# Two-layer encoder trunk: four modulation products moved ahead of attention, and attention 0's norm factors and outputs stored from GpSimd's queue

## Chip, cores and metric

The kernel runs on one core of a Trainium2 chip. The time is device microseconds from launch to end, as the median of three runs. Five engines matter: TensorE (PE in the profile, with its weight loads as PEld), VectorE (DVE), ScalarE (ACT), GpSimd (POOL) and SyncE (SP), which here only issues transfers. Each engine works through its own queue in order. An instruction that waits for a semaphore holds up everything behind it on that engine, also when a transfer is all that the queue issues.

## What is computed

Two pre-norm layers on a sequence of 1024 rows of 1024 features, all in float32. Layer 0 is differential attention with 8 heads, layer 1 multi-head latent attention. Each layer's input is a normalised x, scaled and shifted by a modulation that a conditioning vector c gives; its output passes a gate that c gives as well. Cut to layer 0:

```python
mod = silu(c) @ ada_w + ada_b            # shift, scale, gate: 3 x 1024
h = rmsnorm(x, norm_g) * (1.0 + scale) + shift
q, k, v, z = split(h @ w_in)             # 4 x 1024 columns
q, k = rope(q), rope(k)                  # 16 sub-heads of 64
p = softmax(q1 @ k1.T) - lam * softmax(q2 @ k2.T)   # per head
o = rmsnorm(p @ v, subln_g) * (1 - lambda_init)
x = x + gate * ((o * silu(z)) @ w_out)
```

## The kernel before

**Precision and products.** A float32 operand is split into a high part (ScalarE's cast to float32r) and a low part (a subtraction), and a product is three matmuls: high by high, high by low, low by high (lines 178 to 180). Line 223 makes the high parts of streamed weights on ScalarE, line 224 the low parts on GpSimd. A "k step" is three such matmuls of 128x512.

**The order of layer 0.** First come the normalised input and the first half of the value projection. Then `z0_pair` runs three times: a seven-product (Strassen-like) scheme makes the Q and K projections of heads 2, 4 and 6 from four weight quarters and writes them to DRAM (`rS`); `product0` is one of the seven products, four k steps each. Beside it a list of small jobs, `side`, gives up one entry per k step (`side.tick`; an entry `None` is an empty step), and `side.flush` empties the list at once. In the second run (p == 1) the rotations (rope) of head 0's K and Q are put on this list by `add_jobs` on VectorE: four jobs, each a fetch, two multiplications by the cosine and sine tables, an addition (L390 to L394), a cast on ScalarE (`high`, L398), a subtraction (L403) and stores to `hS`.

At the end of the third run the weights of what follows are split: those of the first streamed projection (`w1`, lines 223 and 224) and the first eight of the second value half's weights (`split_v1`, lines 1077 and 1078), four of them with VectorE and four with GpSimd. Then sixteen k steps of the streamed projections run (`Z_PRE`), then eight value tiles of eight k steps each (`v0_tile`), the seventh with the first scores ahead of it, then attention 0, head by head. A head has eight slots: in each a `q_tile` of scores and softmax (two score matrices, VectorE's maxima at L456, ScalarE's exponentials, VectorE's combination at L1164), the transposes and value products of earlier slots (`Tail`), and three to five k steps of the projections of later heads. `bring` issues the loads of K, Q and V for the next half head; `load_q` has four transfers, two for each of `qa` and `qb` (L844).

**Modulation products.** One of layer 1's sixteen shift and scale columns is a 512 KB load of weights (`ada`) and one VectorE instruction with accumulation over 128x1024 elements (`mod_dot`, L480, "a dot" below). `MODS` says how many are written ahead of each of the eight value tiles: eight in all. The eight others and the eight of the layer's own gate are steps of `gate_steps0`, one of which is taken in every slot from the first of attention 0 on: with one empty step ahead, and the loads of the first two in the second step, the dots are the steps 3 to 18, that is those of heads 0 and 1 and two of head 2. Then follow the gated output weights. The loads share two buffers.

**The norm factors of a half head.** When a half head's values are complete, `close` scales them (`head_out`) and multiplies by the gate (GpSimd, L1226); in the next slot `rest` sums the squares on TensorE, three small VectorE instructions and a power on GpSimd make the factors `y`, 128x4 numbers. `bcast_rows` (line 461) stores them to DRAM (`bc_d`, L464) and reads them back, spread over all partitions (`bc_s`, L466): two transfers in SP's queue. Two slots later GpSimd multiplies the half head by them (`scale`, L1196), and two slots after that SP stores it (`store`, L1200) to `oF`, from which the output projection reads. `hooks` is the list of what is left for the next slot; `after_scores` runs it at its end.

**What sets the order of a queue.** The program is written in one order, but the framework places each engine's instructions and transfers itself: an instruction goes as soon as a plan of the times says that its data and buffers are ready and nothing earlier in the program wants the engine. So instructions written late can be placed early. `in_turn` keeps an instruction in written order among those of its engine that are so marked (from attention 0 on), `behind` and `issue_after` put it behind a given one.

Of the kernel before, what the change touches and what calls it, by code (L numbers as in the profile page):

```python
# [11 lines left out]
F32 = mybir.dt.float32  # L12
# [9 lines left out]
P = 128  # L22
# [4 lines left out]
HF = 512  # L27
# [15 lines left out]
SPL1 = 2  # L43
Z_PRE = 16
V_LATE = 6
MODS = (2, 2, 2, 2, 0, 0, 0, 0)
MODS_K = 0
V1_AT = (3, 3)
NORM_AT = 5
# [35 lines left out]
def trunk(ctx: ExitStack, tc: tile.TileContext, A, out):  # L85
    nc = tc.nc
    SP, PE, V, S, G = nc.sync, nc.tensor, nc.vector, nc.scalar, nc.gpsimd
# [40 lines left out]
    dr = pool(ctx, "dr", bufs=1, space=DRAM)  # L128
# [6 lines left out]
    oF = [dr.tile([NH, 2, P, HF], F32, name=f"oF{l}") for l in range(2)]  # L135
# [49 lines left out]
    def behind(eng):  # L185

        return tc.issue_after(mk[eng]) if eng in mk else nullcontext()

    def in_turn(ins):

        return tc.keep_in_program_order(ins) if mk else ins
# [123 lines left out]
    side = Side()  # L315
# [153 lines left out]
    def t3(ap_):  # L469
        return ap_.rearrange("p (t q) -> p t q", t=4)  # L470
# [26 lines left out]
    def gen_mods(load, c2):  # L497

        for n in range(sum(MODS) + MODS_K):
            src, bias, acc = mod_job(n)  # L500
# [143 lines left out]
    for f in range(2):  # L644
        fs = slice(f * HF, f * HF + HF)
        spread = PE.matmul(cb[:, fs], ones[0:1, :], crow[0:1, fs], start=True, stop=True).ins
# [375 lines left out]
    def z0_pair(p, late):  # L1022
        h, more = FRONT[p], p + 1 < len(FRONT)

        def out(kind, half, t):
            if not kind:
                S.mul(t, t, SC0)
            SP.dma_start(rS[kind][h][half], t)

        if p == 1:  # L1030
            side.flush()
            add_jobs([(kind, 0, half) for kind in (1, 0) for half in range(2)], V, 7)
        u = zt("zu")
        S.copy(u, product0(h0q(0, 0)))
        late(0)
        c_ = zt("z11")
        V.tensor_add(c_, product0(h0q(1, 0)), u)
        out(1, 0, c_)
        late(1)
        v = zt("zv")  # L1040
        S.copy(v, product0(h0q(1, 1)))
        V.tensor_add(u, product0(TK[2]), u)
        u5 = zt("zu5")
        V.tensor_add(u5, product0(TK[1]), u)
        V.tensor_add(v, v, u5)
        out(1, 1, v)
        acc = product0(TK[3])
        c_ = zt("z22")
        V.tensor_add(c_, acc, u5)
        V.tensor_add(u, acc, u)  # L1050
        out(0, 1, c_)
        late(2)
        V.tensor_add(u, product0(TK[4]), u)
        out(0, 0, u)
        late(3)

    def add_jobs(jobs, eng, rest=0):

        jobs = [rot_job(*j, eng) for j in jobs]
        side.add(jobs[0][0], None, None)  # L1060
        for a, b in zip(jobs, jobs[1:] + [[None]]):
            side.add(b[0], None, *a[1:], *[None] * rest)
# [10 lines left out]
    def split_v1(n, eng):  # L1073
        for _ in range(n):
            raw = wvraw.pop(0)
            h_, l_ = tk()
            S.copy(h_, raw)
            eng.tensor_sub(l_, raw, f32v(h_))
            wv1.append((h_, l_))
# [20 lines left out]
    def late(p, i):  # L1100
        if p + 1 < len(FRONT):
            if i < 2:
                z0_fetch(p + 1, ((i, 0), (i, 1)))
            if i == 3 and p + 2 == len(FRONT):
                fetch_v1(4, zrt)
            return
        if i == 0:
            pre.extend(raw_of(*ORDER0[0], f) for f in range(2))
        if i == 1:
            fetch_v1(4, zt)  # L1110
        if i == 2:
            for _ in range(2):
                for a, b in zip(w1, split_raw(pre.pop(0), 4)):
                    a += b
            split_v1(4, V)
        if i == 3:
            split_v1(4, G)

    pre, w1 = [], ([], [])
    for p in range(len(FRONT)):  # L1120
# [47 lines left out]
    for tt in range(8):  # L1168
        if tt == V_LATE:
            psum("ps2", sc=2, tr=1, pv=1)  # L1170
            zz0 = sm.tile([P, 4], F32, name="zz")
            first += [zz0, q_tile(0, 0, 0, zz0, a0a, lambda c: None if c else v0_tile(V_LATE, 1, wv1))]
        for _ in range(MODS[tt]):
            next(mods_g)
# [14 lines left out]

    def finish(o, y, l, h, half, dst, ap_, dgs):  # L1190

        if dst is None:
            b, rb = bcast_rows(ap_, y, "osq", 4)

            def scale():
                in_turn(G.tensor_mul(t3(o), t3(o), rb))  # L1196
                hooks.append(lambda: hooks.append(store))

            def store():
                SP.dma_start(oF[l][h, half], o)  # L1200

            if l == 0:
                hooks.append(lambda: hooks.append(scale))
            else:
                hooks.append(scale)
            return
        rb = bank("z", "rb") if l else Y[1]
        for j in range(4):
            js = slice(j * P, (j + 1) * P)
            S.mul(dgs[:, js], ident, y[:, j : j + 1])  # L1210
            PE.matmul(rb[:, js], ones, dgs[:, js], start=True, stop=True)
        V.tensor_mul(o, o, rb)
# [68 lines left out]
    tails, hooks = [None, None], []  # L1281
# [79 lines left out]
    def gate_steps0():  # L1361

        gcol = sm.tile([P, KT], F32, name="gcol", tag="gcol", bufs=1)
        yield
        w = []
        jobs = [mod_job(n) for n in range(sum(MODS) + MODS_K, 2 * KT)]
        late = len(jobs)
        jobs += [(A["ada_g0"][j], part("ada_bg0")[:, j : j + 1], gcol[:, j : j + 1]) for j in range(KT)]
        for n in range(len(jobs)):
            while len(w) < min(2, len(jobs) - n):  # L1370
                with tc.issue_after(mod_load.last):
                    w.append(mod_load(jobs[n + len(w)][0], pg, 2))
            yield
            with behind("V"):
                mod_dot(w.pop(0), *jobs[n][1:], c2)
                if n == late - 1:
                    g, _, _, a_, _ = mods[1]
                    V.scalar_tensor_tensor(out=a_, in0=a_, scalar=1.0, in1=g, op0=ALU.add, op1=ALU.mult)
        SP.dma_start(gateS[0].rearrange("(p j) -> p j", p=P), gcol)
        yield  # L1380
        SP.dma_start(c2, gateS[0][None, :].to_broadcast([P, D]))
        gb = c2[:, :HF], c2[:, HF:]

        def two(name):
            t = pg.tile([P, D], F32, name=name, tag="ada", bufs=2)
            return t[:, :HF], t[:, HF:]

        def put(*pairs):
            for n, t in pairs:
                SP.dma_start(tS[0][n, h], t)  # L1390

        for h in range(4):
            b_ = (b11, b12), (b21, b22) = two("ob1"), two("ob2")
            for m in range(2):
                for f in range(2):
                    SP.dma_start(b_[m][f], A["w_out0"][f, 4 * m + h])
                yield
            for m in range(2):
                for f in range(2):
                    in_turn(G.tensor_mul(b_[m][f], b_[m][f], gb[f]))  # L1400
                if m:
                    put((0, b11))
                yield
            put((1, b21), (4, b22))
            in_turn(G.tensor_sub(b12, b12, b11))
            t2 = a0c.tile([P, HF], F32, name="ot2", tag="ot2", bufs=2)
            in_turn(G.tensor_sub(t2, b22, b12))
            yield
            put((3, b12), (2, t2))
            in_turn(G.tensor_sub(b11, t2, b11))  # L1410
            in_turn(G.tensor_sub(b21, b21, t2))
            yield
            put((5, b11), (6, b21))
            yield
        for h, wait in ((0, 46), (1, 54)):
            while slot0 < wait:
                yield
            a_ = (a11, a12), (a21, a22) = two("oa1"), two("oa2")
            for m in range(2):
                for f in range(2):  # L1420
                    SP.dma_start(a_[m][f], oF[0][h + 4 * f, m])
                yield
            for _ in combine(a11, a12, a21, a22):
                yield
            SP.dma_start(sS[0][0, h], a22)
            SP.dma_start(sS[0][2, h], a21)
            yield
            SP.dma_start(sS[0][1, h], a11)
            SP.dma_start(sS[0][3, h], a12)
            yield  # L1430
# [94 lines left out]
    class Pre2:  # L1525
        n = 0
# [1049 lines left out]
    def scale(tt, y):  # L2576
        full, early = xs_[tt], tt // 4
        c1, c2_ = halves[early], halves[1 - early]

        def second():  # L2580
            V.scalar_tensor_tensor(out=full[:, c2_], in0=full[:, c2_], scalar=y, in1=fg[:, c2_], op0=ALU.mult, op1=ALU.mult)
            SP.dma_start(out[tt][:, c2_], full[:, c2_])

        def first_():
            S.mul(full[:, c1], full[:, c1], y)
            SP.dma_start(out[tt][:, c1], full[:, c1])

        if tt == NT - 2:
            held.extend((second, first_))
        else:  # L2590
            second()
            first_()
# [160 lines left out]
```

## Time and profile before

| | |
|---|---|
| median of three runs | 1418.11 us (1416.24 to 1419.38) |
| the profiled execution | 1416.81 us, its span 1414.9 us |
| mean granted TensorE clock | 0.991 |
| PE busy | 1369.7 us, 97% of the span |
| DVE / ACT / POOL busy | 1010.1 / 734.5 / 721.1 us |
| transfers | 282.41 MB, mean 200 GB/s |

The profile is of one execution. The times in it start at the span's start. The three `z0_pair` runs lie at about 106 to 171 us, the first streamed projections and the value tiles up to about 233 us, attention 0 from there to about 715 us, its output projection behind it, and layer 1 from about 830 us on. A row of the windows gives for each engine the busy time and the count of instructions in that stretch, a row of the timeline the start, the duration, the engine, the line and the operands, and in brackets the idle time ahead of it and what ended that. Queues that issue transfers have a q behind the engine's name.

### The profile page before, as it was taken

Reading aid. Unit: us, or ns where it says so; the run is one execution under the profiler, and the core shown is the slowest. Engines: PE = TensorE matmul, PEld = TensorE weight load, DVE = VectorE, ACT = ScalarE, POOL = GpSimd, SP = SyncE. Lnnn points to the kernel's source line nnn. Section 1 sums busy time; section 2 is a strip of 40 time slices with the busy share of each in tenths; the row PEclk is TensorE's granted clock in tenths of the full one; section 3 lists DMA queues with packets and bytes.
Section 4 is the critical chain, followed back from the end, with each engine's and each line's share of the span. In section 5 each row is a group of like instructions: output and inputs, shape, how many; then the busy total and the mean of one; then the engine's idle time right before and its main releaser. Section 6 shows DMA issues by size and latency. Waiting matters only on the chain.

```text
span 1414.9 us, 20936 instructions
## 1 busy us (share of the span) xinstructions
PE 1369.7 (97%) x7298; PEld 1141.1 (81%) x7298; DVE 1010.1 (71%) x1414; ACT 734.5 (52%) x1332; POOL 721.1 (51%) x574
## 2 busy tenths in 40 slices
PE   8998899998999999999999999999999999999997
PEld 6786688787888878887787788887888888888886
DVE  7789817999977867888687986645656655555684
ACT  5543314555666655565756553335454454545554
POOL 4424640565688775554785233533141273844673
PEclk8999999999999999999999999999999999999999
DMA  9835778687788776866574236498433354676463
GB/s 341 270 119 179 256 209 282 203 234 236 241 245 250 231 220 202 236 190 198 164 278 165 75 105 210 138 296 262 156 102 120 109 169 159 196 223 196 144 256 120
DMA packets 175243, 282.41 MB, mean 200 GB/s; under 512 B 23457, under 2 KB 60449, under 8 KB 175138
## 3 DMA queue, kind: packets, MB, share of 16 engines
q1 hardware_dynamic: 168610, 266.40, 60.3%
q10 hardware_dynamic: 4608, 8.39, 1.6%
q0 software_dynamic: 1920, 6.29, 1.2%
q8 instruction: 57, 0.93, 0.3%
q14 instruction: 48, 0.39, 0.1%
HBM read 182.49 MB, written 86.98 MB: 190 GB/s over the span
## 4 chain that ended last, share of the span: by engine, by line
PE 71%; DVE 13%; DMA 4%; issue 4%; ACT 4%; POOL 3%; SPq 1%; POOLq 0%; DVEq 0%; ACTq 0%
PE s L2367 10%; PE tr L439 7%; PE acc L180 7%; PE acc L179 6%; PE acc L178 6%; PE s L1156 6%; PE pv L179 4%; PE pv L178 4%; PE pv L180 4%; DVE ada L480 2%; DVE nm L456 2%; DVE e L1164 2%; PE zacc L180 1%; PE zacc L178 1%; PE zacc L179 1%
## 5 line engine op out<-in xcount | busy, mean ns | idle before, releaser
L441 ACT CAST pth<-tr 128x512 fp32r<-128x512 f32 x256 | 150.4, 587 | 247.7 <-PE tr L439 244.8
L442 DVE TENSOR_TENSOR ptl<-tr,pth 128x512 fp32r<-128x512 f32 x256 | 175.9, 687 | 134.5 <-ACT pth L441 129.2
L456 DVE TENSOR_REDUCE nm<-s 128x1 f32<-128x1024 f32 x192 | 233.5, 1217 | 22.0 <-PE s L1156 13.1
L224 POOL TENSOR_TENSOR wl<-wraw,wh 128x512 fp32r<-128x512 f32 (+2 forms) x65 | 84.6, 1302 | 274.5 <-ACT wh L223 249.2
L458 ACT ACTIVATE e<-s,nm 128x1024 f32<-128x1024 f32 x128 | 143.5, 1121 | 63.8 <-DVE nm L456 63.2
L439 PE MATMUL tr<-ident,e 128*128 128x128 f32 x1024 | 155.7, 274 | 8.2 <-DVE ptl L442 7.8
L439 PEld LDWEIGHTS tr<-ident,e 128*128 128x128 f32 x1024 | 120.8, 140 | 50.0 <-DVE ptl L442 28.0
L178 PE MATMUL pv<-pth,vt 128*128 128x256 f32 x512 | 147.8, 289 | 0.0
L179 PE MATMUL pv<-ptl,vt 128*128 128x256 f32 x512 | 147.1, 287 | 0.0
L180 PE MATMUL pv<-pth,vt 128*128 128x256 f32 x512 | 144.6, 282 | 0.0
L178 PE MATMUL acc<-h0h,wh 128*128 128x512 f32 x264 | 108.6, 411 | 0.0
L180 PE MATMUL acc<-h0h,wl 128*128 128x512 f32 x264 | 105.1, 398 | 2.8 <-POOL wl L224 2.8
L179 PE MATMUL acc<-h0l,wh 128*128 128x512 f32 x264 | 105.6, 400 | 0.0
L178 PEld LDWEIGHTS pv<-pth,vt 128*128 128x128 f32 x512 | 97.3, 190 | 3.2 <-ACT pth L441 0.8
L179 PEld LDWEIGHTS pv<-ptl,vt 128*128 128x128 f32 x512 | 97.5, 190 | 2.3 <-DVE ptl L442 0.3
L180 PEld LDWEIGHTS pv<-pth,vt 128*128 128x128 f32 x512 | 97.5, 191 | 0.4
L1503 POOL TENSOR_TENSOR wol<-wol,woh 128x512 fp32r<-128x512 f32 x56 | 82.4, 1494 | 25.5 <-ACT woh L1502 23.9
L1156 PE MATMUL s<-ks,qa 128*128 128x512 f32 x256 | 85.6, 415 | 7.4 <-DVE e L1164 7.1
L1156 PE MATMUL s<-ks,qb 128*128 128x512 f32 x256 | 83.0, 399 | 3.4 <-DMA qb<-hS 3.4
L1164 DVE SCALAR_TENSOR_TENSOR e<-s,z,e 128x1024 f32<-128x1024 f32 x64 | 82.1, 1283 | 1.8
L458 ACT ACTIVATE s<-s,nm 128x1024 f32<-128x1024 f32 x64 | 70.0, 1094 | 13.7 <-DVE nm L456 13.7
L224 POOL TENSOR_TENSOR wl<-zraw,wh 128x512 fp32r<-128x512 f32 (+2 forms) x32 | 46.1, 1447 | 52.3 <-ACT wh L223 40.1
(494 smaller groups left out, 3625.5 us busy)
## 6 DMA issues: line engine op xcount, KB each, us to landing
ada<-in_ada_ss SPq DMA_DIRECT2D x32, 512.0 KB, 5.2
vt<-vS SPq DMA_DIRECT2D x32, 512.0 KB, 5.2
wol<-tS SPq DMA_DIRECT2D x56, 256.0 KB, 5.3
wraw<-in_w_s SPq DMA_DIRECT2D x52, 256.0 KB, 4.2
vS<-v_hl SPq DMA_DIRECT2D x26, 512.0 KB, 5.8
tS<-ob SPq DMA_DIRECT2D x48, 256.0 KB, 3.6
bc_s<-bc_d SPq DMA_DIRECT2D x34, 256.0 KB, 4.0
hS<-rp_sw ACTq DMA_DIRECT2D x32, 256.0 KB, 3.9
```

Of the source, the lines that this page charges most:

```text
L178: PE.matmul(psum, ah, bh, start=first, stop=False, skip_group_check=skip)
L179: PE.matmul(psum, ah, bl, start=False, stop=False, skip_group_check=skip)
L180: mm3.last = PE.matmul(psum, al, bh, start=False, stop=last, skip_group_check=skip).ins
L224: sub = (V if pair_of else G).tensor_sub(l_[:, :n], raw[:, :n], f32v(h_[:, :n]))
L439: transpose_p.last = PE.transpose(tr[:, j, :], p[:, kt * P : (kt + 1) * P], ident).ins
L441: mk["S"] = S.copy(pth[kh][:, :, dst], tr).ins
L442: mk["V"] = V.tensor_sub(ptl[kh][:, :, dst], tr, f32v(pth[kh][:, :, dst])).ins
L456: mk["V"] = V.reduce_max(nm, s_ps, axis=AX.X, negate=True).ins
L458: mk["S"] = S.activation(e, s_ps, AF.Exp, bias=nm, scale=1.0, accum_out=zs).ins
L1156: PE.matmul(s_ps[:, kc * HF : (kc + 1) * HF], src[:, c, ql], KS[h][kc][:, c, :], start=fst, stop=not fst)
L1164: combined.append(V.scalar_tensor_tensor(out=e0, in0=e1, scalar=z1[:, 0:1], in1=e0, op0=ALU.mult, op1=ALU.add).ins)
L2367: PE.matmul(s_ps[:, kc * HF : (kc + 1) * HF], lhs, rhs(kc), start=i == 0, stop=i == 4)
```

## The change

- `MODS` becomes (2, 2, 2, 2, 2, 2, 0, 0): twelve dots are written ahead of value tiles 0 to 5 and four in `gate_steps0`. There, an empty step stands ahead of every second dot of the gate, four in all, so the steps keep their number and the last dot its place.
- Eight empty entries stand ahead of the first rotations on the side list.
- The last four value weights ahead of the tiles are split with VectorE instead of GpSimd.
- For attention 0's half heads (`dst is None and l == 0`: all but the last), `finish` stores the factors from GpSimd's queue, issues the read with `spread` in the next slot instead of at once, multiplies in the slot after that, as before, and stores the result from GpSimd's queue directly behind the multiplication, where SP did so two slots later.

```diff
-MODS = (2, 2, 2, 2, 0, 0, 0, 0)
+MODS = (2, 2, 2, 2, 2, 2, 0, 0)
...
             side.flush()
+            side.add(*[None] * 8)
             add_jobs([(kind, 0, half) for kind in (1, 0) for half in range(2)], V, 7)
...
             split_v1(4, V)
         if i == 3:
-            split_v1(4, G)
+            split_v1(4, V)
...
     def finish(o, y, l, h, half, dst, ap_, dgs):
 
+        if dst is None and l == 0:
+            d_ = dr.tile([HF], F32, name="bc_d", tag="bcd", bufs=4)
+            in_turn(G.dma_start(d_.rearrange("(p t) -> p t", p=P), y))
+
+            def spread():
+                b = ap_.tile([P, HF], F32, name="bc_s", tag="osq", bufs=4)
+                SP.dma_start(b, d_[None, :].to_broadcast([P, HF]))
+
+                def scale():
+                    in_turn(G.tensor_mul(t3(o), t3(o), b.rearrange("p (q t) -> p t q", t=4)))
+                    in_turn(G.dma_start(oF[l][h, half], o))
+
+                hooks.append(scale)
+
+            hooks.append(spread)
+            return
         if dst is None:
             b, rb = bcast_rows(ap_, y, "osq", 4)
...
-            if l == 0:
-                hooks.append(lambda: hooks.append(scale))
-            else:
-                hooks.append(scale)
+            hooks.append(scale)
             return
...
                     w.append(mod_load(jobs[n + len(w)][0], pg, 2))
             yield
+            if n >= late and (n - late) % 2 == 0:
+                yield
             with behind("V"):
                 mod_dot(w.pop(0), *jobs[n][1:], c2)
```

## Prediction

> **What bounds the kernel now.** I read the page's first part, then the busy times by stage, then who PE waits for, and only then the instructions around each wait.
>
> ```profile
> span 1414.9 us, 20936 instructions
> PE 1369.7 (97%) x7298; PEld 1141.1 (81%) x7298; DVE 1010.1 (71%) x1414; ACT 734.5 (52%) x1332; POOL 721.1 (51%) x574
> ```
>
> PE is busy for 1369.7 of 1414.9 us. No edit here takes work from PE, so the change can win only from the 45.2 us in which PE stands still, and from the slow matmuls that follow a long stop. The next two views (columns after the length: busy us and count of PE, PEld, DVE, ACT, POOL, then granted clock, DMA share, GB/s) say where these are.
>
> ```profile
> 120.00:130.00 10.00, 7.29 (x30) 5.04 (x28) 10.00 (x14) 2.19 (x5) 4.46 (x3) 1.00 0.80 263
> 130.00:140.00 10.00, 9.34 (x34) 7.57 (x35) 10.00 (x13) 3.90 (x7) 4.75 (x4) 0.83 0.39 130
> 170.00:180.00 10.00, 7.20 (x25) 5.45 (x24) 10.00 (x10) 2.12 (x5) 8.37 (x5) 0.83 0.37 133
> 180.00:190.00 10.00, 10.00 (x46) 8.27 (x45) 0.80 (x2) 2.43 (x5) 3.83 (x3) 1.00 0.80 237
> ...
> 260.00:372.00 112.00, 102.70 (x584) 84.42 (x583) 106.01 (x146) 63.07 (x115) 67.76 (x55) 1.00 0.78 228
> 372.00:520.00 148.00, 146.95 (x850) 124.65 (x848) 117.47 (x169) 91.35 (x164) 122.62 (x107) 1.00 0.81 243
> 520.00:540.00 20.00, 16.59 (x86) 13.72 (x86) 12.60 (x18) 8.56 (x15) 3.81 (x5) 0.91 0.61 187
> ```
>
> Three places matter. In the products before the values (120 to 180) PE stops and its clock falls to 0.83. In heads 0 and 1 (260 to 372) DVE is busy for 106.01 of 112 us while PE loses 9.3 us. At 520 to 540 PE loses 3.41 us at once. After 372 PE runs almost full, though POOL is busy for 122.62 of 148 us. Each place has its waits:
>
> ```profile
> 128.90 0.50 PE L178 MATMUL zacc<-h0h,wh 128*128 128x512 f32 x1 [1.70 <-ACT wh L223]
> 130.66 0.71 PE L180 MATMUL zacc<-h0h,wl 128*128 128x512 f32 x1 [1.02 <-POOL wl L224]
> ...
> 174.51 0.50 PE L180 MATMUL acc<-h0h,wl 128*128 128x512 f32 x1 [2.80 <-POOL wl L224]
> ...
> 175.46 0.63 PE L180 MATMUL acc<-h0h,wl 128*128 128x512 f32 x1
> 175.89 0.63 PE L178 MATMUL acc<-h0h,wh 128*128 128x512 f32 x1
> ...
> 529.97 1.10 PE L1156 MATMUL s<-ks,qb 128*128 128x512 f32 x2 [3.41 <-DMA qb<-hS]
> ```
>
> (Start, duration, instruction; in brackets the idle time before it and its releaser.) Behind such a stop matmuls start 0.43 us apart (175.46 to 175.89), in a full window about 0.22 (10 us by 46 starts). The second half of the loss in 170 to 180 is this: 25 starts instead of 46 are 4.6 us, and only 2.80 of them idle; I put the slow matmuls at 1.4 us a stop, since a few records can be missing. The stop of 2.80 us so costs 4.2, that of 3.41 us 4.8.
>
> **The change, part by part.**
>
> **A. Four value-weight splits (line 1117) from GpSimd to VectorE.** POOL and ACT at that place:
>
> ```profile
> 169.91 0.61 ACT L223 CAST wh<-wraw 128x512 fp32r<-128x512 f32 x1
> ...
> 168.01 4.77 POOL L1078 TENSOR_TENSOR tk<-wvr,tk 128x512 fp32r<-128x512 f32 x3 [0.85 <-ACT tk L1077]
> 172.75 1.71 POOL L224 TENSOR_TENSOR wl<-wraw,wh 128x512 fp32r<-128x512 f32 x1
> ...
> 168.18 3.48 DVE L1078 TENSOR_TENSOR tk<-wvr,tk 128x512 fp32r<-128x512 f32 x2
> ```
>
> The weight half that PE waits for has its high part from ACT at 170.5; POOL starts its low part at 172.75, because three value splits stand ahead of it. Without them it starts at 170.55 and ends at 171.85 to 172.25 (1.29 us in other rows of POOL, 1.71 here). PE wanted it at 171.71 (174.51 less 2.80), so some 0.8 us of wait is left with the release, and no slow clock: 2.0 + 1.4 = **3.4 us gained** (ends: 0, and 4.2). DVE takes four subtractions, at the 3.48 us of two in this row 7.0 us at most. The cover is DVE's empty time, 0.80 us busy in 180 to 190; the split weights are first read by the value tiles, sixteen k steps (11 us) behind the first projection, and one pair per k step. If that cover were gone, PE would wait for up to the 7.0.
>
> [...]
>
> **B. First rotations eight side entries later (line 1032).** Eight entries are eight k steps of three matmuls, 24 times 0.23 or 5.5 us. What they stand in front of:
>
> ```profile
> 127.71 0.62 ACT L398 CAST rp_sw<-rp_r 128x512 fp32r<-128x512 f32 x1 [6.65 <-DVE rp_r L394]
> 128.23 0.61 ACT L223 CAST wh<-zraw 128x512 fp32r<-128x512 f32 x1
> ```
>
> ACT's queue stood for 6.65 us at the rotation's cast, and the cast of the weight for which PE stopped came right behind. If the rotation moves by 5.5 us and the weight does not, both waits (1.70 and 1.02) and the slow matmuls (1.4) go: 4.1 us. But a queue isn't in the written order: a modulation dot written beside the value tiles ran at 119.41 (row under C). A rotation whose data lie ready can keep its place: then 0. And DVE is busy for all of 120 to 140, so some of the lateness comes back with the next weight. The moved rotations' own loads (four or five issues a job on SP) go with them; the last job now ends behind the last product, and the same free time of DVE covers it. I take **2.0 us gained**, between the ends (0 and 4.1), since the row names the cause while DVE has no room.
>
> **C. Four modulation dots earlier, four empty steps in the gates (lines 46 and 1374).** Sixteen dots ran beside heads 0 and 1, the first eight far ahead of the tiles where they are written:
>
> ```profile
> 119.41 1.27 DVE L480 CUSTOM_DVE_ANT_0 ada<-ada,c,vec 128x1024 f32<-128x1024 f32 x1
> ...
> 192.97 0.69 DVE L419 TENSOR_TENSOR tk<-vps,tk 128x512 fp32r<-128x512 f32 x1 [12.06 <-ACT tk L418]
> ...
> L480 DVE CUSTOM_DVE_ANT_0 ada<-ada,c,vec x16: 1269/1278/4071, 245.6 to 364.2; 128x1024 f32<-128x1024 f32 x16
> ...
> 327.17 4.07 DVE L480 CUSTOM_DVE_ANT_0 ada<-ada,c,vec 128x1024 f32<-128x1024 f32 x1
> ...
> 330.00:340.00 10.00, 7.10 (x45) 5.70 (x44) 9.25 (x13) 5.73 (x10) 4.36 (x3) 1.00 0.67 181
> ```
>
> Twelve stay; by the counting of the steps the freed ones are those of the fifth, eighth, eleventh and fourteenth dot, and the last dot stays at its step. DVE has 4 x 1.28 = 5.1 us less in a stretch where it is 95% busy. A uniform share of PE's 9.3 us, four slots of sixteen, is 2.3; the eleventh dot is the 4.07 one, and the window after it lost 2.90. I take **3.5 us gained** (ends 0 and 5.1; below nothing is excluded, since work leaves the bound engine). The four moved dots need four loads of 512 KB, on SP's queue among the first K and Q loads, and 5.1 us of DVE. DVE stood for 12.06 us before 192.97, and the first scores come six value tiles later (144 matmuls, some 32 us). Without that cover a load costs SP its issue, 0.3 to 0.6 us by the rows under D, and each dot its 1.28.
>
> **D. Norm factors (bc_d) issued by GpSimd, read one slot later; outputs stored by GpSimd (lines 1190 to 1204).** The rows of SP's queue (waits: total us, times, longest):
>
> ```profile
> SPq L464 <- POOL rq_y L1241: 43.2, 11, 10.2
> ...
> 510.89 1.34 SPq L844 DMA_DIRECT2D qa<-hS  x2
> 521.47 0.33 SPq L464 DMA_DIRECT2D bc_d<-rq_y  x1
> 521.90 0.58 SPq L844 DMA_DIRECT2D qb<-hS  x1
> 522.57 0.54 SPq L852 DMA_DIRECT2D zS<-zth  x1
> ...
> 523.64 0.58 SPq L844 DMA_DIRECT2D qb<-hS  x1
> ...
> 523.64 6.28 DMA qb<-hS
> ...
> 519.91 0.68 DVE L851 SCALAR_TENSOR_TENSOR zth<-zth,acc 128x512 f32<-128x512 f32 x1
> ...
> SPq L466 <- DMA bc_d<-rq_y: 8.5, 7, 1.7
> ```
>
> SP stood from 512.2 to 521.5 at one small store; behind it was the query load for which PE stopped at 526.56 (529.97 less 3.41). Without that store both qb loads issue well before, or the second one behind the gate store (zS), whose data DVE has at 520.6. The landing took 6.28 us, so the worse order lands at some 527.3 (520.6, 0.4 to issue, 6.28), 0.7 us late, with no slow clock. Gain 4.8 - 0.7 = **4.1 us** (ends: 0 if SP waits anew, 4.8).
>
> [...]
>
> **E. What GpSimd pays.** Its existing stores show an issue and the wait for its own last result:
>
> ```profile
> L405 POOL DMA_DIRECT2D hS<-rp_raw x24: 582/608/753, 206.0 to 644.4; - x24
> ...
> POOL hS L405 <- POOL rp_raw L403: 7.3, 19, 0.4
> ...
> 691.91 1.29 POOL L1503 TENSOR_TENSOR oal<-oal,oah 128x512 fp32r<-128x512 f32 x1 [2.69 <-ACT oah L1502]
> ```
>
> Fifteen half heads with two stores are thirty issues of 0.61 + 0.38, about 30 us of POOL between 265 and 700. Queued behind them are weight splits, rotations and output scalings. The cover is the distance between a split and its use: 7 to 11 k steps at four a slot of 7 us, so 12 to 19 us. It is gone only in the last head, where POOL splits back to back from 691.91 on and PE follows at once; the two stores of that half head take 2 us there: **2.0 us lost** (ends 0 and 3).
>
> **F. The new wait.** SP's read of the factors (L466) now waits for GpSimd's store to land. It is written behind the query loads of its slot, but SP stays in order; gate stores and swaps stand behind it. I put **1.5 us lost** (ends 0, and 4.8, one stop as at 530).
>
> **The sum** is -3.4 - 2.0 - 3.5 - 4.1 + 2.0 + 1.5 = -9.5 us, from the profiled execution's 1416.81 to 1407.3. The median of the runs, 1418.11, lies 1.3 higher: **1408.6**.
>
> **The rivals.**
>
> 1. *The wait only moves on SP's queue.* L466 is free to be placed as soon as the store is thought to have landed, and POOL is later than the order assumes (11 waits at L464, up to 10.2). SP then stands until POOL's store lands, later than before. For it: SP also waited 8.5 us in all at L466 for its own store. Against: it is written a slot later, behind the query loads. D is lost: 1412.7. [...]
> 2. *The front gives nothing*, so the edit does not do what it says: DVE is full from 120 to 140 and in 170 to 180, and the stops of A and B come back one weight later. 1408.6 + 5.4 = 1414.0.
> 3. *GpSimd becomes the bound: slower.* In 372 to 520 POOL goes from 122.62 to some 133 of 148 us, with waits for late factors on top. From a lag of more than 12 us behind its ACT copies on, each weight split stops PE at 4.2 us. Three such stops, one in every fifth half head, make 12.6: 1421.2. Against, from the page's groups:
>
> ```profile
> L180 PE MATMUL acc<-h0h,wl 128*128 128x512 f32 x264 | 105.1, 398 | 2.8 <-POOL wl L224 2.8
> ```
>
> These matmuls waited 2.8 us for POOL in the whole run, which is the stop of A alone.
>
> **How the numbers follow.** Forecast 0.50, rival one 0.20, rival two 0.17, rival three 0.13. With every end in its favour the sum is -18.2 (1399.9), which asks for everything at once; with rivals one and two together 1418.1. I give 1401 to 1418. A measurement of this kernel tells about 0.2% (2.8 us) from no change. Faster by more: most of the first three cases, 0.77; within: 0.12; slower: 0.11, out of rival three.
>
> **What would show it.** Right: no stop at the first projection's L180 (A) or ahead of the second pair's second product (B); twelve dots after 245; no wait for qb near 525; SP's waits at L464 in attention 0 gone, and PE's loss in 260 to 372 at 6 us or less. Wrong: SP waiting at L466 in the tens of us; PE waits for POOL's wl between 372 and 660; dots or their loads between the K loads and the first scores with PE waiting at 221; a longer last head.

## The result and the profile after

| | before | after |
|---|---|---|
| median, on one chip (runs) | 1418.74 us (4) | 1429.95 us (4) |
| range of the runs | 1416.24 to 1422.22 | 1429.21 to 1432.44 |
| profiled execution, its span | 1416.81, 1414.9 | 1429.41, 1427.6 |
| VectorE's square of the softmax sums (`sl_f`, 16 times): sum, longest | 10.5 us, 1.78 us | 30.2 us, 4.96 us |
| PE's waits for transposed parts (`ptl`): sum, times | 7.8 us, 10 | 14.3 us, 15 |

The ratio is 1.008, with a 95% interval of 1.0055 to 1.0106: the changed kernel is **slower** by 11 us, where 10 us were to be gained. (The median of before is that of the three runs above and one more.) The page and the later stretches of the prediction, now after (same columns):

```profile
PE 1374.6 (96%) x7298; PEld 1143.4 (80%) x7298; DVE 1027.2 (72%) x1418; ACT 733.6 (51%) x1332; POOL 729.7 (51%) x600
```

```profile
170.00:180.00 10.00, 6.64 (x27) 4.54 (x25) 10.00 (x13) 3.20 (x6) 4.65 (x3) 1.00 0.77 267
180.00:190.00 10.00, 8.89 (x32) 7.24 (x33) 3.64 (x7) 2.31 (x4) 5.04 (x3) 0.83 0.91 254
260.00:372.00 112.00, 107.11 (x618) 89.76 (x617) 99.97 (x144) 67.15 (x121) 69.87 (x63) 1.00 0.75 222
372.00:520.00 148.00, 137.07 (x766) 114.07 (x765) 123.64 (x153) 82.20 (x148) 116.69 (x107) 0.98 0.75 229
520.00:540.00 20.00, 20.00 (x120) 17.41 (x119) 15.61 (x25) 11.78 (x21) 12.39 (x12) 1.00 0.54 179
```

The stretch that had a loss of 9.3 us (260 to 372) loses 4.9, and the hole at 520 to 540 is filled. But 372 to 520, which was full, loses 10.9 us, and the slow clock of 0.83 has only moved from 170 to 180 into 180 to 190. The tool for placing a gain is the time at which PE starts its n-th matmul, since PE has the same 7298 in both. Worked out from the two traces (us after less before):

```
matmul            600    700    800   1000   1700   2500   2600   3300   3600   last
before, at us   147.6  177.6  200.8  245.0  377.6  516.6  540.3  659.3  716.1  1407.1
after            -0.4   -3.2   +1.5   +2.0   -3.1  +11.4   +5.7   +7.8  +11.6   +12.9
```

Three stretches gain: 600 to 700 (-2.8), 1000 to 1700 (-5.1) and 2500 to 2600 (-5.7). What they gain is lost right behind two of them, and the large loss is 1700 to 2500, **14.5 us** that no step of the prediction contains. One wait in it, by the timelines of DVE, POOL and PE of the changed kernel:

```profile
405.56 4.53 DVE L1250 TENSOR_TENSOR sl_f<-zz 128x4 f32<-128x4 f32 x1
410.02 0.68 DVE L442 TENSOR_TENSOR ptl<-tr,pth 128x512 fp32r<-128x512 f32 x1
...
403.22 0.60 POOL L1195 DMA_DIRECT2D bc_d<-rq_y  x1 [0.41 <-POOL rq_y L1255]
403.84 1.31 POOL L1421 TENSOR_TENSOR ob<-ob 128x512 f32<-128x512 f32 x1
405.10 1.29 POOL L224 TENSOR_TENSOR wl<-wraw,wh 128x512 fp32r<-128x512 f32 x1
406.33 1.29 POOL L1423 TENSOR_TENSOR ot<-ob,ob 128x512 f32<-128x512 f32 x1
407.58 1.27 POOL L390 TENSOR_TENSOR rp_r<-rp_raw,cosT 128x512 f32<-128x512 f32 x1
408.82 1.25 POOL L393 TENSOR_TENSOR rp_sw<-rp_sw,sinT 128x512 f32<-128x512 f32 x1
410.15 1.27 POOL L394 TENSOR_TENSOR rp_r<-rp_r,rp_sw 128x512 f32<-128x512 f32 x1
...
410.75 0.65 PE L439 MATMUL tr<-ident,e 128*128 128x128 f32 x4 [2.40 <-DVE ptl L442]
```

A multiplication of 128x4 elements, `sl_f`, is 4.53 us "busy". Undisturbed it takes 0.15. It ends at 410.09, when GpSimd pauses for the first time in this row: 408.82 + 1.25 = 410.07, next start 410.15, because line 394 needs the result of line 393. The transposed part behind it on VectorE (`ptl`) starts only at 410.02, and PE stops for 2.40 us. GpSimd's store of norm factors (`bc_d`, 403.22), which the change put there, stands just ahead. The rows of this line, before and after (shortest/median/longest in ns, first and last start; the means are 0.65 and 1.89 us):

```profile
L1236 DVE TENSOR_TENSOR sl_f<-zz x16: 150/634/1781, 251.5 to 694.8; 128x4 f32<-128x4 f32 x16
```

```profile
L1250 DVE TENSOR_TENSOR sl_f<-zz x16: 152/1135/4965, 254.3 to 705.4; 128x4 f32<-128x4 f32 x16
```

### The profile page after: what moved, and what is told of

It reads as the page before. It is cut to its first block, busy times and chain, and to the rows that moved or that the text cites. A ratio compares the mean times of both kernels' runs of the same rounds, so it can differ in the third digit from the quotient of the medians.

```text
span 1427.6 us, 20963 instructions
## 1 busy us (share of the span) xinstructions
PE 1374.6 (96%) x7298; PEld 1143.4 (80%) x7298; DVE 1027.2 (72%) x1418; ACT 733.6 (51%) x1332; POOL 729.7 (51%) x600
## 4 chain that ended last, share of the span: by engine, by line
PE 69%; DVE 13%; issue 5%; DMA 5%; POOL 4%; ACT 3%; SPq 1%; POOLq 0%; ACTq 0%; DVEq 0%
PE s L2383 10%; PE tr L439 6%; PE acc L178 6%; PE acc L180 6%; PE acc L179 6%; PE s L1157 5%; PE pv L178 3%; PE pv L179 3%; PE pv L180 3%; DVE ada L480 2%; DVE sl_f L1250 1%; PE oy L180 1%; PE vps L178 1%; PE oy L179 1%; PE vps L179 1%
## 5 line engine op out<-in xcount | busy, mean ns | idle before, releaser
L439 PE MATMUL tr<-ident,e 128*128 128x128 f32 x1024 | 156.7, 275 | 14.6 <-DVE ptl L442 14.3
```

The costliest lines, as they stand in the source:

```text
L439: transpose_p.last = PE.transpose(tr[:, j, :], p[:, kt * P : (kt + 1) * P], ident).ins
```

## The experiments

The theory to test: after a transfer that GpSimd issues, its next instructions leave VectorE no moment until GpSimd has to wait for something. The rivals: GpSimd is merely too full and late, SP's new wait costs, or the front does. Each run is timed against the kernel before on the same chip (1418.8 to 1419.8 us there).

**1. The square on another engine, in both kernels.** No other engine's order changes.

```diff
-            V.tensor_mul(fin, zz, zz)
+            S.activation(fin, zz, AF.Square)
```

On the changed kernel:

> The changed kernel with the square of the softmax sums (sl_f, 128x4, sixteen times) computed by ScalarE instead of VectorE; the order of all other instructions on every engine stays. Theory 'VectorE is locked out' (its 4-element product waits up to 4.96 us for GpSimd's stream, and the transposes behind it wait for ptl): sl_f takes under 0.3 us, the PE waits 'tr <- DVE ptl' fall from 12.7 us in all to 7 or less, most of the 14.5 us lost between about 375 and 528 us comes back, time 1414 to 1421. Rival 'GpSimd is simply too full' (late factors and late splits): the loss stays, 1427 to 1430. Rival 'the stores' DMA traffic slows the loads': also 1427 to 1430.

On the kernel before, as a control:

> The kernel before with the same single edit, as a control. Lockout theory: there sl_f took 0.63 us on average (1.78 at most), 10.5 us in all instead of 30.2, so little is to be had: 0 to -4 us, 1415 to 1419. Rival 'moving the square off VectorE is worth the same anywhere': -10 or more, 1409 or less.

Measured: **1414.98 us** (ratio to before 0.9975, 0.996 to 0.999) and 1419.14 (0.9995, 0.9979 to 1.001). The same edit is worth 15 us behind the change and nothing ahead of it. PE's waits for `ptl` fall from 14.3 to 4.0 us (the 12.7 of the expectation are those of attention 0 alone), and from the 1700th to the 2500th matmul the kernel now loses 3.8 us, not 14.5. So most of that loss hangs on this one instruction on VectorE; that a transfer of GpSimd's is what holds it up is for experiment 3 to show. Of the 3.8 us that stay, 2.1 are a stop of PE for an exponential, behind a rotation that GpSimd finishes late.

**2. The change cut in two: D alone, and A, B and C alone.** The first is the kernel before with the new branch of `finish`; the second is the changed kernel with that branch out and lines 1202 to 1205 of before in again.

> The kernel before with only part D of the change (norm factors and outputs of attention 0 issued by GpSimd, factors read a slot later). Theory: D carries the loss, +14.5 between the 1700th and 2500th matmul, about +3 in the last head, less the stop for qb (-5.7): 1428 to 1434, with sl_f near 1.9 us on average. Rival 'D is neutral and the front (A, B) loses': 1417 to 1420.

> The changed kernel with part D undone, so A, B and C alone. Theory: C gains 5 us, A loses about 2, B nothing: 1413 to 1418. Rival 'the front loses': 1424 or more.

Measured: D alone **1435.86** (1.0119, 1.009 to 1.0148), worse than the whole change and above the 1428 to 1434 expected, with `sl_f` at 20.1 us in all (mean 1.26 us, not the 1.9 expected). So `sl_f` isn't all that D costs there: between the 1000th and the 1700th matmul, where all sixteen dots still run, its trace loses 8.3 us, and the cause of that stays open. A, B and C alone **1422.43** (1.0012, 0.9998 to 1.0026), not the 1413 to 1418 expected: `sl_f` is down to 7.3 us and D carries the loss, but the front's gain isn't there either. Where it went is experiment 6.

**3. One store more, one wait more.** If the issue of a transfer is what matters, a useless store from GpSimd must bring the loss back in the kernel with D undone; and a pair of tiny dependent multiplications behind the real store, at which GpSimd has to wait for itself, must take it away.

```diff
             in_turn(G.tensor_mul(y, y, fin))
+            x_ = dr.tile([HF], F32, name="bx_d", tag="bxd", bufs=4)
+            dst is None and in_turn(G.dma_start(x_.rearrange("(p t) -> p t", p=P), y))
```

> The changed kernel with part D undone (1422.4 us), and one more store of the norm factors from GpSimd's queue to a buffer that nothing reads, behind the factors' last product. Nothing waits for it. Theory (GpSimd's DMA issue ahead of the stream): sl_f rises from 0.46 to between 1.2 and 2.0 us on average with cases over 3 us, and the time to 1428 to 1436. Rival 'D loses by the wait for GpSimd's factors or by SP': sl_f stays below 0.7, time 1421 to 1425.

```diff
             in_turn(G.dma_start(d_.rearrange("(p t) -> p t", p=P), y))
+            r_ = sm.tile([P, 4], F32, name="ral")
+            in_turn(G.tensor_mul(r_, y, y))
+            in_turn(G.tensor_mul(r_, r_, y))
```

> The changed kernel with two more 4-element multiplications on GpSimd behind each store of norm factors (bc_d), the second needing the first's result; their result is used by nothing. Theory 'after a DMA issue of its own GpSimd runs its next instructions without a moment in which VectorE's two-input product gets in, until GpSimd has to wait for a result of its own': the pair makes such a wait right behind the store, so sl_f falls from 1.89 to 1.3 us or less on average, none over 2, and the time to 1413 to 1420, although GpSimd has about 0.5 us more to do per store (some 8 us in all). Rival 'GpSimd is too busy or too late, and sl_f merely falls into its full stretches': sl_f stays near 1.9 or grows, time 1429 to 1434.

Measured: the useless store **1433.10** (1.009, 1.0062 to 1.0118), `sl_f` from 7.3 to 29.1 us; the pair **1419.44** (0.9997, 0.9979 to 1.0015), `sl_f` from 30.2 to 12.4 us, 10.5 us faster with more work on GpSimd. Same place, the kernel with D undone first (timelines of POOL and DVE):

```profile
496.27 1.03 POOL L174 TENSOR_TENSOR rq_y<-sl_w,mhalf 128x4 f32<-128x4 f32 x1
497.38 0.20 POOL L1242 TENSOR_TENSOR rq_y<-rq_y,sl_f 128x4 f32<-128x4 f32 x1
497.53 2.54 POOL L1403 TENSOR_TENSOR ob<-ob,c 128x512 f32<-128x512 f32 x2
...
498.68 0.18 DVE L1237 TENSOR_TENSOR sl_f<-zz 128x4 f32<-128x4 f32 x1
```

and with the useless store:

```profile
501.10 0.60 POOL L1242 DMA_DIRECT2D bx_d<-rq_y  x1 [0.40 <-POOL rq_y L1242]
501.72 2.52 POOL L1403 TENSOR_TENSOR ob<-ob,c 128x512 f32<-128x512 f32 x2
504.21 1.28 POOL L390 TENSOR_TENSOR rp_r<-rp_raw,cosT 128x512 f32<-128x512 f32 x1
505.46 1.26 POOL L393 TENSOR_TENSOR rp_sw<-rp_sw,sinT 128x512 f32<-128x512 f32 x1
506.80 1.26 POOL L394 TENSOR_TENSOR rp_r<-rp_r,rp_sw 128x512 f32<-128x512 f32 x1
...
501.79 4.95 DVE L1237 TENSOR_TENSOR sl_f<-zz 128x4 f32<-128x4 f32 x1
```

In the first, GpSimd paused for its own result at 497.30 to 497.38, and `sl_f` gets in between the two halves of line 1403, which follow each other without a pause. In the second the same two halves and two more boundaries let nothing in. With the pair behind the real store:

```profile
401.35 0.60 POOL L1195 DMA_DIRECT2D bc_d<-rq_y  x1 [0.41 <-POOL rq_y L1255]
401.98 0.21 POOL L1195 TENSOR_TENSOR ral<-rq_y 128x4 f32<-128x4 f32 x1
402.27 0.20 POOL L1195 TENSOR_TENSOR ral<-ral,rq_y 128x4 f32<-128x4 f32 x1
402.42 1.28 POOL L1421 TENSOR_TENSOR ob<-ob 128x512 f32<-128x512 f32 x1
403.66 1.30 POOL L224 TENSOR_TENSOR wl<-wraw,wh 128x512 fp32r<-128x512 f32 x1
404.92 1.30 POOL L1423 TENSOR_TENSOR ot<-ob,ob 128x512 f32<-128x512 f32 x1
...
403.70 1.27 DVE L1250 TENSOR_TENSOR sl_f<-zz 128x4 f32<-128x4 f32 x1
```

The pause is at 402.19 to 402.27, and `sl_f` gets in at the next boundary (404.96), though GpSimd goes on there without a pause. One `sl_f` still took 3.48 us, against the expectation: a rotation's addition had slipped in between the two small ones, so the second had nothing left to wait for.

**4. Which of the two stores.** The norm factors back on SP's queue:

```diff
-            in_turn(G.dma_start(d_.rearrange("(p t) -> p t", p=P), y))
+            SP.dma_start(d_.rearrange("(p t) -> p t", p=P), y)
```

> The changed kernel with the norm factors stored from SP's queue again; the outputs stay on GpSimd's. Theory: the store ahead of sl_f is gone, so sl_f is 0.4 to 0.8 us; SP waits for the factors as before (40 us or more in all), and a stop for qb of 3 to 5 us can come back: 1415 to 1424. Rival 'the thirty issues and 0.4 us waits on GpSimd are the cost': half of the loss stays, 1424 to 1428.

The outputs back on SP's queue, two slots later:

```diff
-                    in_turn(G.dma_start(oF[l][h, half], o))
+                    hooks.append(lambda: hooks.append(lambda: SP.dma_start(oF[l][h, half], o)))
```

> The changed kernel with the outputs stored from SP's queue, two slots later as before; the norm factors stay on GpSimd's. Theory: the store ahead of sl_f stays, so sl_f stays near 1.9 us and the time near the changed kernel's: 1425 to 1431. Rival 'the outputs' stores on GpSimd are the cost': 1415 to 1421.

Measured: factors on SP **1420.66** (1.0003, 0.9987 to 1.0019), `sl_f` 7.6 us; outputs on SP **1424.37** (1.0037, 1.002 to 1.0054), `sl_f` 30.6 us. The lockout goes with the factors' store. The outputs' store has a cost of its own, some 5.6 us against the changed kernel: that run came out below the 1425 that the theory gave, though `sl_f` takes as long as in the changed kernel. No stop of PE for `qb` came back near 530 us with the factors on SP, against the expectation.

**5. Parts A and the last heads, on the kernel with the square on ScalarE.** A undone (`split_v1(4, G)` again); then also the last head's factors and outputs the old way; then the last two heads' with A as in the change. The branch in the last one (the second has `NH - 1`):

```diff
-        if dst is None and l == 0:
+        if dst is None and l == 0 and h < NH - 2:
...
-            hooks.append(scale)
+            hooks.append((lambda: hooks.append(scale)) if l == 0 else scale)
```

> The changed kernel with the square on ScalarE (1415.0 us) and part A undone: the four value-weight splits back on GpSimd. Theory (moving them only moves the stop: VectorE, full, then empties the product's bank late and PE waits for zu): the stop for zu of 2.8 to 3.4 us goes, the one for wl of 2.8 comes back, and the time falls by 1 to 3 us, to 1412 to 1414.5. Rival 'A gains as predicted': the time rises by 2 to 4 us, to 1417 to 1419.

> The same kernel as the one before it in this set, and the last head's two half heads store norm factors and outputs from SP's queue as before. Theory (in the last head GpSimd stands at the output's scaling until the factors are back, and the splits behind it reach PE late): the stops for oal and wol (2.7 and 1.5 us) fall to 0.5, and the time is 3 to 5 us below that of the one before it, 1408 to 1411. Rival 'the last head's loss is its issues only': less than 1.5 us better.

> The changed kernel with the square on ScalarE, and the norm factors and outputs of the last two heads stored from SP's queue as before. With the last head alone that way the stop for oal stayed (3.2 us), behind an output scaling of the head before, at which GpSimd stood 8 us for its factors. Theory (that scaling is in GpSimd's order ahead of the last head's splits, and its factors come later by way of GpSimd's own store): now the stop for oal falls to 0.5 us, the loss from the 3300th to the 3400th matmul (3.8 us with the square alone) to 1 or less, time 1411 to 1414. Rival 'PE merely comes earlier, and the splits wait for data that do not come forward': the stop for oal stays at 2.5 to 4 us, time 1414 to 1417.

Measured: **1416.63** (0.9983, 0.997 to 0.9995), **1418.03** (0.9988, 0.9976 to 1.0) and **1410.18** (0.993, 0.9905 to 0.9956). The first lies between its two expectations and can't be told from 1414.98, so what A costs or brings by the clock stays open; in the trace the stop for `wl` is back (2.8 us), and the one for `zu` falls to 0.24. The second refutes the theory as put: the last head's own stores weren't the cause, the stop for `oal` stays at 3.2 us. The third finds it one head earlier, and comes out 0.8 us below the range expected. GpSimd with the square alone, then with the last two heads the old way:

```profile
669.47 1.55 POOL L1202 TENSOR_TENSOR o<-o,bc_s 128x512 f32<-128x512 f32 x1 [7.51 <-DMA bc_s<-bc_d]
671.42 0.59 POOL L1203 DMA_DIRECT2D oF<-o  x1 [0.41 <-DMA wol<-tS]
672.03 2.51 POOL L1519 TENSOR_TENSOR oal<-oal,oah 128x512 fp32r<-128x512 f32 x2
```

```profile
668.28 1.55 POOL L1213 TENSOR_TENSOR o<-o,bc_s 128x512 f32<-128x512 f32 x1 [6.98 <-DMA bc_s<-bc_d]
669.97 1.27 POOL L1519 TENSOR_TENSOR oal<-oal,oah 128x512 fp32r<-128x512 f32 x1
```

The split that PE waits for starts 2.06 us earlier: 1.19 because the factors arrive earlier, the rest because the issue (0.59) and the idle time ahead of it (0.41) are gone. This row puts the 0.41 down to a load; at eleven others of these stores the trace puts it down to the scaling's own result. PE's stop for it falls from 2.7 to 0.5 us. This version beats both kernels, by 8.7 us the one before.

**6. C alone.** The kernel before with the two edits of part C.

> The kernel before with part C alone (four modulation dots earlier, four empty steps). Theory (C gains some 5 us up to the 1700th matmul, but with the norm factors on SP's queue the reload of a rotation's rows then comes late and PE stops near 415 for exp behind the rotation's cast): 12 dots after 245 us, a gain of 3 to 6 us at the 1700th matmul, some 4 to 7 us lost again near 415, time 1416 to 1421. Rival 'C gains and keeps it': 1412 to 1415.

Measured: **1418.89** (0.9993, 0.998 to 1.0005). From the 1000th to the 1700th matmul it gains 5.0 us in the trace, as in the changed kernel, and by the 2500th 2.6 are lost again, less than the 4 to 7 expected, most of it in two stops near 415 and 419 us (1.5 for an exponential, 0.6 for VectorE's combination). The stop for `qb` near 530 us stays (3.1 us, 3.4 before). What else is missing was lost earlier: at the 1000th matmul this trace is already 3.6 us behind that of before, and no run shows why. The same place near 415 in the run of A, B and C shows the chain in full (issues of SP, then POOL, ACT and PE):

```profile
405.23 0.33 SPq L464 DMA_DIRECT2D bc_d<-rq_y  x1
405.61 0.53 SPq L383 DMA_DIRECT2D rp_raw<-rS  x1
...
410.92 1.29 POOL L390 TENSOR_TENSOR rp_r<-rp_raw,cosT 128x512 f32<-128x512 f32 x1 [1.85 <-DMA rp_raw<-rS]
...
415.35 0.62 ACT L398 CAST rp_sw<-rp_r 128x512 fp32r<-128x512 f32 x1 [4.81 <-POOL rp_r L394]
...
417.63 0.80 PE L1157 MATMUL s<-ks,qa 128*128 128x512 f32 x1 [3.54 <-ACT e L458]
```

SP stands at the norm factors, behind them the reload of a rotation's rows issues at 405.61, GpSimd rotates late, the rotation's cast holds ScalarE's queue for 4.81 us, and the exponential behind it comes late for PE. This is the same kind of wait on SP that D was to remove, at another place: PE, earlier by C, runs into it. It isn't the whole cause. With the factors off SP's queue and the square on ScalarE (experiment 1) the rotation's rows come in time, and PE still stops there for 2.10 us for the exponential, behind the same cast (3.39 us of wait for GpSimd). All this is read from the traces and was not tried by itself.

One execution's trace is not exact to a few us: the control of experiment 1, whose time is that of before, lies 5 us behind the profile of before in its own.

## Why the prediction was wrong

The measured time lies above the whole predicted range of 1401 to 1418 us. By the prediction's own steps, with the changed kernel's gain or loss in the stretch of matmuls where the step works (each figure is of one execution):

| step | predicted, us | measured, us | matmuls |
|---|---|---|---|
| A four splits to VectorE (the +4.7 together with C's dots) | -3.4 | -2.8, then +4.7 | 600 to 700, to 800 |
| B rotations later | -2.0 | 0 | up to 600 |
| C dots earlier | -3.5 | -5.1 | 1000 to 1700 |
| D stores off SP's queue | -4.1 | -5.7 | 2500 to 2600 |
| E GpSimd's issues, last head | +2.0 | +3.8 | 3300 to 3600 |
| F new wait on SP | +1.5 | no stop found | |
| (not in it) mostly the lockout of VectorE | 0 | +14.5 and +2.1 | 1700 to 2500, 2600 to 3300 |

- **The step that failed is E** ("Queued behind them are weight splits, rotations and output scalings"): it counted what an issue takes from GpSimd and who queues behind it on GpSimd, and not what it does to a VectorE instruction beside GpSimd. It bounded the thirty issues between 0 and 3 us. The factors' store alone costs 9 to 11 us in experiments 3 and 4, and the square that it holds up 15 us in experiment 1. (Of the 14.5 and 2.1 us in the table's last row, 3.8 and 0.8 stay when the square is on ScalarE.) The prediction had the clue in its hands, the dot of 4.07 us at 327.17. GpSimd beside it, before:

```profile
324.26 0.58 POOL L405 DMA_DIRECT2D hS<-rp_raw  x1 [0.30 <-POOL rp_raw L403]
324.87 1.29 POOL L224 TENSOR_TENSOR wl<-wraw,wh 128x512 fp32r<-128x512 f32 x1
326.11 1.55 POOL L1196 TENSOR_TENSOR o<-o,bc_s 128x512 f32<-128x512 f32 x1
327.63 1.27 POOL L390 TENSOR_TENSOR rp_r<-rp_raw,cosT 128x512 f32<-128x512 f32 x1
328.87 1.29 POOL L393 TENSOR_TENSOR rp_sw<-rp_sw,sinT 128x512 f32<-128x512 f32 x1
```

  The dot waited through three of GpSimd's instructions and got in at none of the boundaries near 327.65 and 328.9, with a store ahead of them all. The prediction used its 4.07 us only to place C's gain.
- **A**: mechanism right, and the next late thing missed. The stop for the low part fell from 2.80 to 0.65 us, but behind it PE needs a bank that VectorE empties, and VectorE does that no earlier than before. The timelines of PE and DVE after, and DVE's before:

```profile
172.44 0.50 PE L180 MATMUL acc<-h0h,wl 128*128 128x512 f32 x1 [0.65 <-POOL wl L224]
181.10 0.80 PE L178 MATMUL acc<-h0h,wh 128*128 128x512 f32 x1 [3.40 <-DVE zu L1054]
...
176.97 1.27 DVE L480 CUSTOM_DVE_ANT_0 ada<-ada,c,vec 128x1024 f32<-128x1024 f32 x1
...
178.17 2.27 DVE L480 CUSTOM_DVE_ANT_0 ada<-ada,c,vec 128x1024 f32<-128x1024 f32 x1
...
180.37 0.68 DVE L1054 TENSOR_TENSOR zu<-zacc,zu 128x512 f32<-128x512 f32 x1
```

```profile
175.53 1.70 DVE L480 CUSTOM_DVE_ANT_0 ada<-ada,c,vec 128x1024 f32<-128x1024 f32 x1
...
180.22 0.69 DVE L1053 TENSOR_TENSOR zu<-zacc,zu 128x512 f32<-128x512 f32 x1
```

  The stop comes back with its slow clock (0.83 in 180 to 190). VectorE's instruction ahead of the two dots starts earlier than before (line 1051 at 176.37; line 1050 of before, the same one, at 179.44), but then the dots run, 3.5 us in all, and only then the one that empties the bank. Before, one dot stood in this stretch. With C alone the second is there too (at 178.45), so the stop belongs to A and C together: without A it falls to 0.24 us (experiment 5), and no run has A without C. The cover named for A ("DVE's empty time" in 180 to 190) lay behind this instruction, not ahead of it. VectorE also waited beside GpSimd: the second dot took 2.27 us against 1.27 of the first, beside a subtraction of GpSimd's (177.70 to 179.35), but that is only a part of the stop.
- **B**: zero, as rival two had it. PE's stop for `wh` is still 1.74 us (1.70 before), behind the same cast with 6.63 us of wait (6.65):

```profile
128.55 0.50 PE L178 MATMUL zacc<-h0h,wh 128*128 128x512 f32 x1 [1.74 <-ACT wh L223]
...
127.36 0.62 ACT L398 CAST rp_sw<-rp_r 128x512 fp32r<-128x512 f32 x1 [6.63 <-DVE rp_r L394]
```

  Up to 164 us every engine does its work in the same order in both traces: the eight entries moved nothing.
- **C and D**: right in place, larger than forecast. Twelve dots run after 245, as counted, and no wait for `qb` is left near 525. Moving the four dots took more off VectorE than the 5.1 us counted: the twelve that stay take 18.8 us in all, the sixteen took 27.2, since some had waited (4.07, 2.80 and 2.55 us the longest). But C alone, and A, B and C together, gain nothing by the clock (experiments 2 and 6), so the two terms don't look independent, as the sum took them. In the four traces with C and the factors still stored from SP, C's stretch gains 0.3 to 5.1 us, in the seven others 4.3 to 7.9; that fits, and isn't shown by a run of its own. For D, the factors' store need not leave SP: in experiment 4 it is back there, and both `qb` loads issue ahead of it (519.26 against 529.36), so no stop comes. What counts in these traces is that the loads don't stand behind a wait.
- **E's own term**: +3.8 instead of +2.0; the last heads' scaling waits for factors, which the prediction didn't follow.
- **F and rival one**: the wait moved as rival one has it, from 43.2 us at line 464 to 57.2 at the new read:

```profile
SPq L1199 <- DMA bc_d<-rq_y: 57.2, 15, 18.5
```

  but between 233 and 720 us PE has no stop for a load. D's gain was not lost there, so rival one's price was wrong. (GpSimd's wait for the factors themselves, in the last heads, is counted under E.)
- **Rival two** holds for A and B: between the first and the 800th matmul the changed kernel gains nothing.
- **Rival three** had the sign and the engine and not the way: between 233 and 720 us the profile shows no wait of PE for a projection's low part (line 224), where 12.6 us were priced. GpSimd didn't fall behind PE, it kept VectorE out.

The stop at 530 went, 5.7 us in its stretch, and the trace of before has the reason: a semaphore wait of 9.2 us on the issuing queue (SP's, up to the factors' store at 521.47), with the `qb` loads behind it (521.90 and 523.64).

## What to carry to other kernels

Before work or a store goes to GpSimd, look at the VectorE instructions beside it, small ones above all: the profile shows a lockout as an instruction whose longest is many times its shortest (the square 0.15 to 4.96 us behind the change, the dots 1.27 to 4.07 before it, where `ptl` takes 0.67 to 0.69 between 240 and 735 us in both). When a transfer has to be issued from GpSimd, let GpSimd wait for a result of its own right behind it (here for 10.5 us), or move the VectorE instruction that it holds up to another engine (here to ScalarE, for 15 us). And a stop removed ahead of a full engine is worth only the distance to that engine's next deadline: find that instruction's end in the trace before counting the gain.

## What the runs showed of the hardware

- **A transfer issued by GpSimd lengthens the lockout of VectorE.** Over all fourteen traces, between 240 and 735 us, I took each square or dot that waited at least 0.25 us, and each boundary inside the wait at which GpSimd went on within 0.05 us. Where GpSimd had issued a transfer since its last pause, VectorE got in at 0 of 72 such boundaries; where it had paused since, at 20 of 20. (At four more boundaries GpSimd went on with another transfer's issue; VectorE got in at three of them.) A pause is any gap over 0.05 us, by a wait for a result of its own (0.08 us is enough) or of another engine.
- Where GpSimd had paused, the wait ended with the instruction of GpSimd's that was running: the five such waits in the trace of before lasted 0.46 to 0.74 us (the time of the instruction less its shortest). Behind a transfer the blocking spans up to four instructions of GpSimd's, 4.96 us (500.03 in the changed kernel). What holds VectorE out there, no run shows.
- The same edit can be worth nothing on one kernel and 15 us on its successor: moving `sl_f` to ScalarE gave 0.9995 of the time before the change, and 1414.98 us instead of 1429.95 behind it.
